# First stage of a transformer layer: modulation and first features as one list schedule, second shift by GpSimd products and ScalarE sums, no transposes of modulation weights

## The chip, the cores and the metric

One core of one Trainium2 chip runs the whole program. The metric is device microseconds of one execution, median of several. The engines are named as in the profile: PE (TensorE matmuls) and PEld (its weight loads), DVE (VectorE), ACT (ScalarE), POOL (GpSimd), SP (SyncE, which issues most DMAs).

## The reference

One layer of a diffusion backbone on 512 latent and 256 context tokens of width 2048, all in float32. What this change touches is the beginning:

```
mod_x = silu(c) @ w_ada + b_ada          # 6 x 2048 numbers: shift, scale, gate, twice
mod_c = silu(c_ctx) @ w_ada + b_ada
h  = rmsnorm(x)   * norm1_w * (1 + scale_x) + shift_x      # latent tokens
hc = rmsnorm(ctx) * norm1_w * (1 + scale_c) + shift_c      # context tokens
p  = h @ w_in;  pc = hc @ w_in
```

Differential attention (8 heads), latent attention (8 heads), the output projection, a gated MLP with a convolution and a last norm follow. The change computes the same numbers.

## The kernel before

Activations stand with features on the 128 partitions and tokens along the free axis: 16 tiles x of 128x512 (latent) and 8 tiles of 128x512, each with two context tiles of 128x256. A tile index is called kt (0 to 15). Float32 products are made from a high part (float32r) and a remainder: `split` copies the high part on ACT (L217) and subtracts on DVE (L218), and `mm3` makes three matmuls, high by high, high by low, low by high (L241 to L243).

The stage in question runs from the start to the end of the first five output tiles, the "first features":

1. Loads of x and ctx (L415, L418). ACT squares them (L435, L437), DVE squares half of the context (L439) and adds all squares up (L441); one matmul with ones sums over partitions (L448) and `rstd` (L293 to L302) gives the reciprocal root `rinv`.
2. silu(c) and silu(c_ctx) are spread over all partitions as `cb` and `ccb` by matmuls with ones (L429) and copies (L443, L445).
3. `modulation(u)` for a pair of tiles, u from 0 to 7. `scales(u)`: 16 matmuls of the padded columns `cpad` with the weight columns `adak` in four column groups of PE (L348), an eviction (L350), two small matmuls with `sel` that add the groups (L352), and L360 on DVE, which gives the factors `a1`. `shifts(kt)`: for an even kt a dot product along the free axis on DVE for c and one for c_ctx, each in two halves of 1024 (L384, an operation that also reads its accumulator); for an odd kt the weight rows `ada` are transposed on PE (L400, 16 of 128x128), evicted by ACT (L401), multiplied as in `scales` and evicted to `modx`, `modc` (L404). The weights of the first features are loaded and split (L227, L217, L218).
4. For each kt: DVE scales the tile (L500), ACT adds the shift and rounds to the high part (L502), DVE makes the remainder (L503), for the latent and for the context tile; then PE makes 27 matmuls (five latent outputs and four context outputs, three each).

Item 1 and 2 are in an order written out by hand; items 3 and 4 are ordered by the framework's priorities. The PSUM of the stage is full: two tiles of two banks and four of one; one of them, `acc`, serves all of modulation.

The attention that comes later is ordered by a planner, the class `Flow`: each step has an engine, a cost, a due time `at` and the buffers it reads and writes; a table `PLAN` shifts the due times of named parts; `run` walks through time, gives each free engine the ready step that is due first, and then emits the steps in that order. Buffers of a ring are given out in order of due times.

Of the kernel before, what the change touches and what calls it, by code (L numbers as in the profile page):

```python
# [9 lines left out]
F32 = mybir.dt.float32  # L10
# [41 lines left out]
class Buf:  # L52


    def __init__(self, flow, ring, make):
        self.ring, self.make, self.tile = ring, make, None
        self.users, self.writers, self.readers, self.left = [], [], [], 0
# [7 lines left out]
class Step:  # L65
    __slots__ = ("eng", "cost", "lag", "at", "fn", "bufs", "left", "next", "takes", "start", "n", "ready")

    def __init__(self, eng, cost, lag, at, fn, n):
        self.eng, self.cost, self.lag, self.at, self.fn, self.n = eng, cost, lag, at, fn, n
        self.bufs, self.left, self.next, self.takes, self.ready = [], 0, [], [], 0.0  # L70
# [10 lines left out]


class Flow:
# [7 lines left out]
    def buf(self, make, ring=None, count=None):  # L91
        if ring and ring not in self.rings:
            self.rings[ring] = (count, [])
        return Buf(self, ring, make)

    def step(self, eng, cost, at, fn, r=(), w=(), needs=(), lag=None):
        at += self.plan.get(self.part, 0.0)
        s = Step(eng, cost, self.LAGS[eng] if lag is None else lag, at, fn, len(self.steps))
# [6 lines left out]
        for b in dict.fromkeys([*r, *w]):  # L105
            if b.ring and not b.users:
                s.takes.append(b)
            b.users.append(s)
            b.left += 1
            s.bufs.append(b)  # L110
# [10 lines left out]
    def run(self):  # L121
# [4 lines left out]
        engines = {"PE": -3.0, "ACT": 2.0, "DVE": 2.8, "POOL": 0.0, "SP": now, "X": -3.0}  # L126
# [6 lines left out]

        for s in self.steps:
            if not s.left:
                event(s.ready)
                open_[s.eng].append(s)
        order = []

        turns = {}  # L140
        for s in sorted(self.steps, key=lambda s: (s.at, s.n)):
            for b in s.takes:
                turns.setdefault(b.ring, []).append(b)

        def free(b):
            count, taken = self.rings[b.ring]
            if turns[b.ring][len(taken)] is not b:
                return False
            return len(taken) < count or taken[-count].left == 0

        event(now)
        for t in set(engines.values()):
            event(t)
        while events:
# [4 lines left out]
            for s in batch:  # L159
                if s is None:  # L160
                    continue
                for b in s.bufs:
                    b.left -= 1
                for n_ in s.next:
# [6 lines left out]
            for e in engines:  # L171
                while engines[e] <= now + 1e-9:
                    can = [s for s in open_[e] if s.ready <= now + 1e-9 and all(free(b) for b in s.takes)]
# [4 lines left out]
                    for b in s.takes:  # L178
                        self.rings[b.ring][1].append(b)
# [10 lines left out]
def layer_kernel(ctx: ExitStack, tc: tile.TileContext, small, rope, c_row, cc_row, x_t, ctx_t, ada, ada_k,  # L190
# [56 lines left out]
    sm.tile([P, 88], F32, name="edge")  # L247
# [77 lines left out]


    zero_d = dram.tile([64, TT], F32, name="zero_d")
# [4 lines left out]
    for c0, c1, r in ((0, 480, slice(0, 64)), (480, TT, slice(64, P))):  # L332
        gp.dma_start(zero_d[:, c0:c1].rearrange("p (k j) -> p k j", j=(c1 - c0) // KT),
                     cpad[r, :, 2:2 + (c1 - c0) // KT])
# [7 lines left out]
    def products(src, n):  # L342


        for j in range(4):
            for c in range(4):
                kt = 4 * j + c
                pe.matmul(acc[32 * c:32 * c + 32, :n], cpad[:, kt], src(kt), start=j == 0, stop=j == 3)  # L348
        row = st.tile([P, 2 * P], F32, tag="row", name=nm("row"), bufs=1)[:, :n]
        sc.copy(row, acc[:, :n])  # L350
        for i in range(n // P):
            pe.matmul(acc[:, 2 * i:2 * i + 2], row[:, i * P:(i + 1) * P], sel, start=True, stop=True)  # L352

    def scales(u, ws=None):

        ws = ws or columns(u)
        products(lambda kt: ws[kt // 4][:, kt % 4], 2 * P)
        for i in range(2):
            kt = 2 * u + i
            ve.tensor_scalar(out=a1[:, 2 * kt:2 * kt + 2], in0=acc[:, 2 * i:2 * i + 2], scalar1=b1[:, kt:kt + 1],  # L360
                             scalar2=col("n1", kt), op0=ALU.add, op1=ALU.mult)

    def columns(u):
        ws = []
        for j in range(4):
# [21 lines left out]
    def shifts(kt):  # L387
# [4 lines left out]
        if kt % 2 == 0:  # L392
            for i in range(2):
                shift(kt, ws, i)
# [1463 lines left out]
```

## Time and profile before

| | |
|---|---|
| median of 3 runs | 2398.79 us (2398.31 to 2403.32) |
| the profiled execution | 2404.97 us |
| its span on the core | 2403.1 us, 33008 instructions |
| PE busy | 2342.3 us (97%) |
| DVE busy | 1701.1 us (71%) |
| ACT busy | 1153.6 us (48%) |
| POOL busy | 336.3 us (14%) |
| DMA | 404.31 MB, mean 168 GB/s |

A row of a group reads: line, engine, operation, output<-inputs, shapes, count, then busy time and mean ns of one, then the idle time of the engine just before and what ended it. A row of a stretch reads: from:to in us, its length, the busy time and the count of each engine, then the granted clock of PE (1.00 is full), the busy share of the DMA engines and GB/s. A row in order of time reads: start, duration, engine, line, operation. An instruction that is issued and then held counts as busy while it is held.

### The profile page before, as it was taken

The numbers are of one execution on the slowest core, as the hardware profiler recorded it, in microseconds if no ns is written. First come the engines' busy times: TensorE is split into PE (matmuls) and PEld (weight loads), VectorE is DVE, ScalarE is ACT, GpSimd is POOL, SyncE is SP. The second block draws the span as 40 slices with busy tenths as digits, with TensorE's granted clock in tenths as the row PEclk, the third lists the DMA queues.
The fourth block names the chain that finished last, engine by engine and source line by source line (L and its number), as shares of the span: only waits on it lengthen the run. The fifth ranks groups of instructions, "written<-read, shape, count | busy, mean of one in ns | idle before, by whom it ended". The sixth has DMA issues, their size and how long they took to land.

```text
span 2403.1 us, 33008 instructions
## 1 busy us (share of the span) xinstructions
PE 2342.3 (97%) x12758; PEld 1981.3 (82%) x12758; DVE 1701.1 (71%) x2244; ACT 1153.6 (48%) x1752; POOL 336.3 (14%) x320
## 2 busy tenths in 40 slices
PE   5999999999999999999999999999999999999997
PEld 3678878887788888798888888888888888888887
DVE  6668886477878766399585757575767676766767
ACT  4333121177776732255454545454545444544546
POOL 0000000155433221100101010101010101111110
PEclk9999999999999999999999999999999999999999
DMA  8867899844521168333646465555554656565573
GB/s 281 295 230 277 304 336 330 269 130 139 156 64 50 34 255 320 131 115 97 144 130 144 128 144 137 140 140 141 132 147 123 153 122 158 123 153 128 140 186 105
DMA packets 132853, 404.31 MB, mean 168 GB/s; under 512 B 14628, under 2 KB 25380, under 8 KB 124244
## 3 DMA queue, kind: packets, MB, share of 16 engines
q1 hardware_dynamic: 106166, 351.66, 44.4%
q0 software_dynamic: 25376, 49.49, 11.9%
q8 instruction: 100, 1.64, 0.3%
q10 hardware_dynamic: 1152, 1.05, 0.1%
q14 instruction: 59, 0.48, 0.1%
HBM read 332.47 MB, written 69.67 MB: 167 GB/s over the span
## 4 chain that ended last, share of the span: by engine, by line
PE 84%; DVE 7%; DMA 4%; ACT 3%; issue 2%; SPq 0%; DVEq 0%; ACTq 0%
PE y L1577 12%; PE b L242 10%; PE b L241 10%; PE b L243 9%; PE z L1577 6%; PE y L1579 6%; PE s L241 3%; PE s L719 3%; PE s L243 3%; PE s L242 3%; PE z L1579 3%; DMA ada<-in_ada 3%; PE x L1577 2%; PE f L241 1%; PE f L242 1%
## 5 line engine op out<-in xcount | busy, mean ns | idle before, releaser
L1598 POOL DMA_DIRECT2D x_d<-xs x160 | 139.9, 1005 | 1161.4 <-ACT xs L1597 1159.5
L1433 DVE TENSOR_TENSOR wl<-wr,wh 128x1024 fp32r<-128x1024 f32 x144 | 176.5, 1225 | 158.6 <-ACT wh L1425 157.9
L1425 ACT CAST wh<-wr 128x1024 fp32r<-128x1024 f32 x144 | 151.1, 1049 | 234.8 <-PE b L242 120.7
L241 PE MATMUL b<-ah,wh 128*128 128x512 f32 (+1 forms) x664 | 256.8, 387 | 0.0
L242 PE MATMUL b<-al,wh 128*128 128x512 f32 (+1 forms) x664 | 256.7, 387 | 0.0
L243 PE MATMUL b<-ah,wl 128*128 128x512 f32 (+1 forms) x664 | 255.9, 385 | 0.0
L1433 DVE TENSOR_TENSOR wl<-rb,wh 128x1024 fp32r<-128x1024 f32 x123 | 150.0, 1220 | 126.8 <-ACT wh L1425 126.8
L1425 ACT CAST wh<-rb 128x1024 fp32r<-128x1024 f32 x123 | 129.3, 1051 | 186.5 <-PE b L242 115.8
L1433 DVE TENSOR_TENSOR wl<-ws,wh 128x1024 fp32r<-128x1024 f32 x123 | 150.1, 1221 | 89.8 <-ACT wh L1425 89.8
L1425 ACT CAST wh<-ws 128x1024 fp32r<-128x1024 f32 x123 | 128.3, 1043 | 130.1 <-PE b L242 45.2
L309 DVE CUSTOM_DVE_ANT_0 ada<-ada,cb,smt 128x2048 f32<-128x2048 f32 x64 | 152.3, 2383 | 46.6 <-DMA ada<-in_ada 46.6
L1577 PE MATMUL y<-a2k,wh 128*128 128x512 f32 x656 | 164.0, 392 | 0.0
L217 ACT CAST wh<-wr 128x1024 fp32r<-128x1024 f32 (+1 forms) x69 | 67.5, 978 | 195.2 <-PE s L243 48.8
L241 PE MATMUL b<-a2k,wh 128*128 128x512 f32 (+1 forms) x376 | 141.7, 377 | 5.9 <-ACT a2k L1282 4.3
L243 PEld LDWEIGHTS b<-ah,wl 128*128 128x128 f32 x664 | 124.8, 188 | 25.7
L241 PEld LDWEIGHTS b<-ah,wh 128*128 128x128 f32 x664 | 125.1, 188 | 22.9
L242 PEld LDWEIGHTS b<-al,wh 128*128 128x128 f32 x664 | 125.1, 188 | 22.0
L242 PE MATMUL b<-a2k,wh 128*128 128x512 f32 (+1 forms) x376 | 140.9, 375 | 0.0
L243 PE MATMUL b<-a2k,wl 128*128 128x512 f32 (+1 forms) x376 | 140.1, 373 | 0.0
L1577 PEld LDWEIGHTS y<-a2k,wh 128*128 128x128 f32 x656 | 118.6, 189 | 21.6
L218 DVE TENSOR_TENSOR wl<-wr,wh 128x1024 fp32r<-128x1024 f32 (+1 forms) x69 | 80.0, 1159 | 46.0 <-ACT wh L217 45.5
L722 DVE TENSOR_REDUCE m<-s 128x1 f32<-128x768 f32 x96 | 91.2, 951 | 28.0 <-PE s L719 27.5
(480 smaller groups left out, 5932.5 us busy)
## 6 DMA issues: line engine op xcount, KB each, us to landing
ada<-in_ada SPq DMA_DIRECT2D x64, 1024.0 KB, 7.0
rb<-in_w_up SPq DMA_DIRECT2D x123, 512.0 KB, 4.3
wr<-in_w_dn SPq DMA_DIRECT2D x88, 512.0 KB, 4.1
x_d<-xs POOLq DMA_DIRECT2D x160, 256.0 KB, 6.0
wr<-in_w_up SPq DMA_DIRECT2D x53, 512.0 KB, 4.2
wr<-in_w_f SPq DMA_DIRECT2D x34, 512.0 KB, 7.3
ada<-in_ada SPq DMA_DIRECT2D x32, 512.0 KB, 7.2
adak<-in_ada_k SPq DMA_DIRECT2D x32, 512.0 KB, 6.3
```

What stands on the lines that cost most here:

```text
L218: ve.tensor_tensor(dst_l, src, dst_h.bitcast(F32), op=ALU.subtract)
L241: pe.matmul(out, st[0], mv[0], start=start, stop=False, **kw)
L242: pe.matmul(out, st[0], mv[1], start=False, stop=False, **kw)
L243: pe.matmul(out, st[1], mv[0], start=False, stop=stop, **kw)
L309: ve.tensor_tensor_reduce(out=junk, in0=w, in1=vec, op0=ALU.mult, op1=ALU.add, scale=1.0, scalar=col("b_ada", j), accum_out=dst[:, j:j + 1])
L719: pe.matmul(s()[:, c0:c1], a, b[:, c0:c1], start=i == 0, stop=i == len(ms) - 1)
L722: step("DVE", 0.87, t + cost + 0.2, lambda: ve.tensor_reduce(out=m(), in_=s()[:, :TT], axis=AX.X, op=ALU.max, negate=True), r=[s], w=[m])
L1425: sc.copy(t, raw[:, k * n_:k * n_ + n_])
L1433: ve.tensor_tensor(t, raw[:, k * n_:k * n_ + n_], hi[k].bitcast(F32), op=ALU.subtract)
L1577: pe.matmul(o, w[j][0], hs[j], start=start and j == 0, stop=False, skip_group_check=True)
L1579: pe.matmul(o[:, h0], w[j][1], hs[j][:, h0], start=False, stop=j == 7, skip_group_check=True)
L1598: gp.dma_start(x1_d[dt], x, accum_op=ALU.add)
```

## The change

**One planned stage.** Items 1 to 4 above become steps of a `Flow` of their own (`flow.part` names: l loads, b spreading, q squares, r the root, a scales, d and p the two shifts, k features), with costs and due times as numbers in the code: T0 = 31 and 6.15 us for each kt. The table `PLAN` has new entries for these parts and changed entries for the attention parts. `Flow.run` takes the engines' starting times as an argument, and a ring's buffer is now given out when any buffer of the ring is free, in order of due times, not when the one that is `count` places back is free.

**The second shift.** For c (shift of the latent tokens) every kt has the dot product on DVE, in two halves. For c_ctx only kt = 0 has it; for kt 1 to 15 POOL multiplies the weight rows by `ccb` in two halves of 128x1024 into tiles `pj` (a ring of 2), ACT sums each along the free axis (an identity with an accumulator), and one small DVE operation adds the halves and `b_ada`. Transposes, their evictions and the second set of products on PE are gone.

**Smaller pieces.** POOL squares the context tiles (16 of 128x256); the last two squares are not added on DVE but go into the matmul with ones; the root's refinement is done for latent and context tokens apart; four copies to `cb` move to ACT and four to `ccb` to DVE; the table of ACT for exp and the small exp stand earlier; the zeros `zero_d` are written from a zeroed tile behind this stage, as rows of 768, and no longer from `cpad` at the start in pieces of 30 and 18 numbers; a padding tile `edge` shrinks from 88 to 24 columns, and the sums `sh` take 64.

The core of the diff:

```diff
+    def shift(kt):
+        ws = rows[kt]
+        t = T0 + PER * kt - 12
+        for i in range(2):
+            at_b[i][kt] = b = buf(lambda: None)
+            d, vec = (modx, modc)[i][:, kt:kt + 1], (cb, ccb)[i]
+            flow.part = f"{'dp'[i]}{kt}"
+            if i and kt:
+                parts_ = []
+                for hf in range(2):
+                    pj = buf(lambda: st.tile([P, 1024], F32, tag="pj", name=nm("pj"), bufs=2), "pj", 2)
+                    o, a = slice(hf * D // 2, (hf + 1) * D // 2), buf(lambda: None)
+                    step("POOL", 2.5, t + 2.5 * hf, lambda hf=hf, pj=pj, o=o: gp.tensor_tensor(
+                        out=pj(), in0=ws[hf](), in1=ccb[:, o], op=ALU.mult), r=[ws[hf], *wide[1]], w=[pj])
+                    step("ACT", 1.0, t + 2.5 * hf + 2.5, lambda hf=hf, pj=pj: sc.activation(
+                        pj(), pj(), AF.Identity, accum_out=sh[:, 2 * kt + hf:2 * kt + hf + 1]), w=[pj, a], lag=0.3)
+                    parts_.append(a)
+                step("DVE", 0.15, t + 6.3, lambda d=d: ve.scalar_tensor_tensor(
+                    out=d, in0=sh[:, 2 * kt:2 * kt + 1], scalar=col("b_ada", kt), in1=sh[:, 2 * kt + 1:2 * kt + 2],
+                    op0=ALU.add, op1=ALU.add), r=parts_, w=[b])
+                continue
+            for hf in range(2):
+                def dot(hf=hf, i=i, d=d, vec=vec):
+                    w = ws[hf]()
+                    junk = st.tile([P, D // 2], BF16, tag="junk", name=nm("junk"), bufs=1)
+                    ve.tensor_tensor_reduce(out=junk, in0=w, in1=vec[:, hf * D // 2:(hf + 1) * D // 2], op0=ALU.mult,
+                                            op1=ALU.add, scale=1.0, scalar=d if hf else col("b_ada", kt), accum_out=d)
+
+                step("DVE", 1.3, t + 3 + 1.3 * hf + 2.6 * i, dot, r=[ws[hf], *wide[i]], w=[b], lag=0.2)
...
-        wt = st.tile([P, KT, P], F32, tag="wt", name=nm("wt"), bufs=1)
-        for q in range(4):
-            for i in range(4):
-                k = (q % 2) * 4 + i
-                pe.transpose(acc[:, i * P:(i + 1) * P], ws[q // 2][:, k * P:(k + 1) * P], ident)
-            sc.copy(wt[:, 4 * q:4 * q + 4].rearrange("p k f -> p (k f)"), acc)
-        products(lambda kt: wt[:, kt], P)
...
+        step("POOL", 0.75, t, lambda q=q, c=c, o=o: gp.tensor_tensor(out=q()[:, T:], in0=c()[:, o], in1=c()[:, o],
+                                                                   op=ALU.mult), r=[c], w=[q])
...
+        flow.run({"PE": 1.0, "ACT": 3.8, "DVE": 5.0, "POOL": 2.0, "SP": 1.0, "X": 0.0})
...
-        flow.run()
+        flow.run({"PE": -3.0, "ACT": 2.0, "DVE": 2.8, "POOL": 0.0, "SP": -100.0, "X": -3.0})
```

How the order moves. POOL's program of before, from its first own instructions on (`ident` is the identity, `cpad` the padded columns, `v_d` the stored values of the attention):

```order
masks.py:197 MEMSET ident 128x128
L331 MEMSET cpad 128x512
masks.py:199 ISA
masks.py:199 AFFINE_SELECT ident<-ident 128x128
L333 DMA zero_d<-cpad 64x16x30
L333 DMA zero_d<-cpad 64x16x18
L652 DMA v_d_137<-v_3770 128x4x128
```

And POOL's program of the change, where the squares of the context (`h` from `c2k`) give way to the products (`pj` from weight rows `ada` and the spread `ccb`):

```order
L418 TENSOR_TENSOR h_319<-c2k_276 128x256
L418 TENSOR_TENSOR h_327<-c2k_276 128x256
L520 TENSOR_TENSOR pj_375<-ada_342,ccb 128x1024
L520 TENSOR_TENSOR pj_392<-ada_350,ccb 128x1024
L520 TENSOR_TENSOR pj_408<-ada_365,ccb 128x1024
L520 TENSOR_TENSOR pj_434<-ada_380,ccb 128x1024
```

POOL had nothing between zero_d's writes and the stored values; now it has 16 squares and 30 products there, and zero_d's write stands behind them.

DVE's program of before, in the middle of the stage, one pair of tiles: `wl` are remainders of weights, `a2k` and `c2k` of features, `h` scaled tiles, ISA is the dot product and the reading of its accumulator:

```order
L218 TENSOR_TENSOR wl_642<-wr_639,wh_641 128x640
L218 TENSOR_TENSOR wl_694<-wr_691,wh_693 128x640
L384 ISA junk_775,modx<-ada_771,cb,smt 128x1024
L384 ISA modx 128x1
L384 ISA ada_771,modc<-ada_771,ccb,smt 128x1024
L384 ISA modc 128x1
L384 ISA junk_777,modx<-ada_773,cb,modx 128x1024
L384 ISA modx 128x1
L404 TENSOR_SCALAR modx<-b_334,smt 128x1
L404 TENSOR_SCALAR modc<-b_334,smt 128x1
```

The same place in the change:

```order
L533 ISA junk_793,modx<-ada_743,cb,modx 128x1024
L533 ISA modx 128x1
L533 ISA junk_805,modx<-ada_760,cb,modx 128x1024
L533 ISA modx 128x1
L475 TENSOR_TENSOR wl_818<-wr_772,wh_803 128x640
L525 SCALAR_TENSOR_TENSOR modc<-sh,smt 128x1
L556 SCALAR_TENSOR_TENSOR h_831<-a2k_213,a_91,rinv 128x512
L561 SCALAR_TENSOR_TENSOR a2k_842<-h_788,modx,a2k_823 128x512
L556 SCALAR_TENSOR_TENSOR h_788<-c2k_207,a_91,rinv 128x256
L533 ISA junk_858,modx<-ada_795,cb,smt 128x1024
```

Every dot is now one with `cb` into `modx`, for even and odd tiles; `modc` comes from the sums `sh` by one small operation.

PE's program of before, between the first features of two tiles (`wh` and `wl` weights, `b` and `s` PSUM tiles; `ident` marks the transposes):

```order
L400 MATMUL b_334<-ident,ada_645 128x128 x4
L242 MATMUL b_331<-a2k_736,wh_521 128x512
L243 MATMUL b_331<-a2k_735,wl_522 128x512
L241 MATMUL s_425<-a2k_871,wh_641 128x512
L241 MATMUL s_426<-a2k_871,wh_641 128x512
L400 MATMUL b_334<-ident,ada_645 128x128 x4
L242 MATMUL s_425<-a2k_872,wh_641 128x512
```

And in the change:

```order
L488 MATMUL b_322<-adak_525,cpad 32x256 x4
L247 MATMUL s_422<-a2k_554,wh_510 128x512
L248 MATMUL s_422<-a2k_571,wh_510 128x512
L249 MATMUL s_422<-a2k_554,wl_534 128x512
L488 MATMUL b_322<-adak_539,cpad 32x256 x4
```

Between features only the matmuls for the scales are left.

More of the change, by code (lines that the diff above doesn't have):

```diff
@@ L119, in step, with run @@
         return s
-    def run(self):
+    def run(self, begin):
         import heapq
         now = -100.0
-        engines = {"PE": -3.0, "ACT": 2.0, "DVE": 2.8, "POOL": 0.0, "SP": now, "X": -3.0}
+        engines = dict(begin)
         open_ = {e: [] for e in engines}
@@ L138, in run @@
         order = []
[L140 to L143, printed above, removed]
         def free(b):
[L146 to L153, printed above, removed]
+            return not b.ring or b.taken or turns[b.ring][0] is b and live[b.ring] < self.rings[b.ring]
         while events:
@@ L172, in run @@
                 while engines[e] <= now + 1e-9:
-                    can = [s for s in open_[e] if s.ready <= now + 1e-9 and all(free(b) for b in s.takes)]
+                    can = [s for s in open_[e] if s.ready <= now + 1e-9 and all(free(b) for b in s.bufs)]
                     if not can:
@@ L354, in scales @@
[L354 to L365, printed above, removed]
-            wk = st.tile([P, 4, 2 * P], F32, tag="adak", name=nm("adak"), bufs=4)
-            nc.sync.dma_start(wk, ada_k[u, j // 2][:, (j % 2) * 4:(j % 2) * 4 + 4])
-            ws.append(wk)
-        return ws
@@ new lines, in layer_kernel @@
+    for kt in range(KT):
+        features(kt)
+    flow.part = "l"
+    load(T0 + 30, 200, lambda: nc.sync.dma_start(ropet, rope), [buf(lambda: None)])
+    step("SP", 0.4, T0 + 20, lambda: nc.sync.dma_start(silu_c, cb[0:1]), r=[rows_[0]])
+    with tc.manual_schedule(engines={mybir.EngineType.PE, mybir.EngineType.Activation, mybir.EngineType.DVE,
+                                     mybir.EngineType.SP, mybir.EngineType.Pool}):
+        flow.run({"PE": 1.0, "ACT": 3.8, "DVE": 5.0, "POOL": 2.0, "SP": 1.0, "X": 0.0})
@@ L510, in layer_kernel @@
+    lat0, ctx0 = [lat0(f) for f in range(5)], [ctx0(f) for f in range(4)]
     st.release()
```

365 lines of the change are left out of this document (226 added, 139 removed), and 21 rows, old and new, of the table PLAN.

## The prediction

> **What bounds the kernel now.** I read the profile from the whole to the place. The section on the 40 slices shows TensorE (PE) at 90% or more in all but the first and the last; the change works in the first three. So the next view was the busy time by stretches, cut where the stages change.
>
> ```profile
> core 0: us, PE busy (x) PEld busy (x) DVE busy (x) ACT busy (x) POOL busy (x), PEclk, DMA share, GB/s
> 0.00:35.00 35.00, 14.02 (x16) 5.15 (x16) 20.21 (x38) 20.46 (x33) 3.07 (x9) 1.00 0.95 284
> 49.00:184.00 135.00, 132.93 (x1073) 95.44 (x1072) 86.78 (x169) 50.56 (x98) 0.00 (x0) 0.98 0.74 263
> ```
>
> For 35 us PE waits for inputs and their squares; from 49 to 184 us it is busy for 132.9 of 135 us, while VectorE (DVE) has 86.8 us of work and GpSimd (POOL) none. The chain that ended last and PE's instructions in order of time give the two edges:
>
> ```profile
> 34.26 0.96 DVE sqs L441
> 35.26 2.92 PE s L448 x4
> ...
> 49.30 1.22 PE s L241 x2
> ```
> ```profile
> 183.71 0.39 PE L243 MATMUL b<-a2k,wl 128*128 128x512 f32 x1
> ```
>
> The stage is over at 183.71 + 0.39 = **184.1 us**. What follows, down to the end at 2403.1, starts from there, so the change is worth what it does to this number. PE's modulation work in the stage, grouped by form:
>
> ```profile
> L400 PE MATMUL b<-ident,ada 128*128 128x128 f32 x128 | 22.0, 298 | 4.0 <-issue 2.0 <-ACT wt L401 1.4 <-DVE a L360 0.6
> L348 PE MATMUL b<-adak,cpad 128*32 128x256 f32 x256 | 21.2, 415 | 0.0
> L348 PE MATMUL b<-wt,cpad 128*32 128x128 f32 x256 | 9.5, 294 | 0.0
> ...
> L352 PE MATMUL b<-sel,row 128*128 128x2 f32 x48 | 6.7, 233 | 1.0 <-ACT row L350 1.0
> ```
> ```profile
> 94.59 0.57 PE b L348 x8
> ...
> 111.36 0.57 PE b L348 x8
> ```
>
> **What the change takes from PE.** The transposes (22.0 us), the products on transposed weights (9.5) and 8 of the 24 small matmuls behind them (a third of 6.7) go: about 33 us that stood on the bounding engine, 4.2 of the 16.8 us that a pair of feature tiles takes (the last two rows, from the chain, open successive pairs). On ScalarE (ACT) the evictions of those transposes go; 30 sums over 128x1024 come. The write of zero_d moves from the first microseconds behind the stage, where no one needs it for 200 us.
>
> **What it adds.** Thirty products of 128x1024 on POOL (L520), two for each of the feature tiles 1 to 15, and 16 squares of 128x256. DVE keeps its load: it loses the second dot product of 7 even tiles and gains the first of 8 odd ones (34 dots of 1024 instead of 32), its 16 splits of weights, 64 feature operations and most of the additions of squares. In the stage of before POOL never ran, so whether the two engines can work side by side has to be read further on, where both run. There the rows speak plainly. DVE, then POOL, at 883 us:
>
> ```profile
> 883.16 2.34 DVE L309 CUSTOM_DVE_ANT_0 ada<-ada,cb,smt 128x2048 f32<-128x2048 f32 x1
> ...
> 885.43 2.30 DVE L218 TENSOR_TENSOR wl<-wr,wh 128x1024 fp32r<-128x1024 f32 x1
> 887.65 3.38 DVE L309 CUSTOM_DVE_ANT_0 ada<-ada,cb,smt 128x2048 f32<-128x2048 f32 x1
> ```
> ```profile
> 883.45 3.20 POOL L1152 TENSOR_TENSOR ss<-ss,sq 128x512 f32<-128x512 f32 x1
> ...
> 887.16 1.72 POOL L1152 TENSOR_TENSOR ss<-ss,sq 128x512 f32<-128x512 f32 x1
> ```
> ```profile
> L1152 POOL TENSOR_TENSOR ss<-ss,sq x11: 1292/1724/3199, 881.4 to 973.6; 128x512 f32<-128x512 f32 x11
> ```
>
> POOL's sum takes 1.29 us at best, here 3.20: it starts at 883.45, the dot product ends at 885.50, the sum ends at 886.65, that is 1.15 later. The split L218, begun at 885.43, ends at 887.73, 1.08 behind POOL's end. Then POOL again 1.15 behind that, and the next dot at 891.03, 2.15 behind 888.88. They take **strict turns**, and each counts what it costs behind the other's end. The same with the wider form and with the short ones:
>
> ```profile
> L871 POOL TENSOR_TENSOR p<-p,p x32: 1833/1850/2484, 485.0 to 667.3; 128x768 f32<-128x768 f32 x32
> ```
> ```profile
> 519.13 2.48 POOL L871 TENSOR_TENSOR p<-p,p 128x768 f32<-128x768 f32 x1 [0.29 <-ACT p L870]
> ```
> ```profile
> 518.62 1.30 DVE L683 TENSOR_TENSOR wl<-wr,wh 128x1024 fp32r<-128x1024 f32 x1
> 519.83 0.95 DVE L722 TENSOR_REDUCE m<-s 128x1 f32<-128x768 f32 x1
> 521.03 0.69 DVE L702 TENSOR_TENSOR wtl<-pt,wth 128x512 fp32r<-128x512 f32 x1 [0.25 <-ACT wth L695]
> ```
>
> POOL's 128x768 sum waits for the split's end at 519.92 and ends 1.69 later (alone: 1.83 at best). The reduction L722 and L702, whose inputs lie in PSUM, wholly or in part, run beside it at their usual length. So those DVE instructions block that read two tensors from SBUF, and in this stage that is nearly all of them: the dots (L533), the splits (L475), the feature products and remainders (L556, L561), the additions of squares (L423).
>
> Here the Trainium skill disagrees with itself, and the choice decides the sign. "Advanced Engine Details and Errata", section Mode Summary, names only DVE's instructions in a 2-port mode as those that GpSimd blocks; by that sentence alone the dots would run beside the products, and the result would be the first rival below. "SBUF — State Buffer", section SBUF: two separate sides, adds instructions with two SBUF inputs and says that the pair is held for the whole instruction; the sum would then be the one that follows. The rows above agree with the second: 3.20 and 3.38 us instead of 1.29 and 2.34.
>
> **The sum of the shared turns.** DVE's prices alone, from its groups in the stage of before:
>
> ```profile
> L441 DVE TENSOR_TENSOR sqs<-sqs,sq 128x768 f32<-128x768 f32 x15 | 14.3, 956 | 2.2 <-ACT sq L437 1.2
> L218 DVE TENSOR_TENSOR wl<-wr,wh 128x640 fp32r<-128x640 f32 x16 | 13.2, 822 | 1.1 <-ACT wh L217 0.9
> L503 DVE SCALAR_TENSOR_TENSOR a2k<-h,modx,a2k 128x512 fp32r<-128x512 f32 x16 | 12.0, 748 | 1.8 <-ACT a2k L502 1.8
> L500 DVE SCALAR_TENSOR_TENSOR h<-a2k,a,rinv 128x512 f32<-128x512 f32 x16 | 11.2, 745 | 0.0
> L384 DVE CUSTOM_DVE_ANT_0 junk<-ada,cb,modx 128x1024 bf16<-128x1024 f32 x8 | 10.3, 1283 | 0.1
> ...
> L503 DVE SCALAR_TENSOR_TENSOR c2k<-h,modc,c2k 128x256 fp32r<-128x256 f32 x16 | 7.7, 479 | 0.5 <-ACT c2k L502 0.5
> ...
> L384 DVE DVE_READ_ACCUMULATOR2_ANT modx<- 128x1 f32 x16 | 1.3, 84 | 0.0
> ```
>
> POOL's 128x1024 product is in no row. Its two forms step by 0.54 us per 256 columns (1.15 to 1.69 behind a wait, 1.29 to 1.83 alone), so an estimate is 2.25 behind a wait and 2.39 alone; the 128x256 square is 0.60 or 0.74 in the same way. DVE behind a wait: 1.08 for 1024 columns gives, in proportion, 0.82 (768), 0.69 (640), 0.55 (512), 0.28 (256) and 1.08 for a dot of half 2048.
>
> - Low end, everybody behind a wait: 13 additions 10.7, 16 squares 9.6, 34 dots 36.7, 16 splits 11.0, 32 wide and 32 narrow feature operations 26.6, the six of the root's refinement 2.5, 30 products 67.5: **165 us**.
> - High end, everybody at its price alone: 12.4, 11.8, 34 x (1.28 + 0.08) = 46.2, 13.2, 39.2, 2.9, 71.7: **197 us**.
>
> DVE has some 130 such instructions and POOL 46, so only about a third of DVE's stand behind a wait: DVE's 113.9 less a third of the 26.4 between its ends is 105, and 7 less for successive instructions that overlap by 0.08: 98. POOL lies in the middle of its ends, 80. Together **178 us**.
>
> This starts when the first x tile lands. ACT squares it at 10.3 us now, while zero_d's small pieces fill the DMA engines (share 0.81 at 170 GB/s in the first 10 us); without them I take 8, and it can hardly be before 5.
>
> ```profile
> 0.00:10.00 10.00, 2.79 (x4) 1.23 (x5) 1.15 (x11) 6.14 (x5) 3.07 (x9) 1.00 0.81 170
> ...
> 30.00:40.00 10.00, 4.74 (x24) 2.14 (x28) 8.44 (x12) 5.69 (x11) 0.00 (x0) 1.00 1.02 408
> 40.00:50.00 10.00, 6.03 (x38) 3.69 (x31) 7.23 (x14) 4.06 (x9) 0.00 (x0) 0.72 0.33 117
> 50.00:60.00 10.00, 10.00 (x73) 7.81 (x71) 7.45 (x17) 2.38 (x5) 0.00 (x0) 0.77 1.01 366
> ```
>
> Three small terms: 8 us in which the pair is free because DVE waits for ACT's high part (0.66 us at 178 us now) once for each of 8 pairs of tiles, or for a load; 5 us at the end, since PE now ends 4.9 us behind the last L503; and 5 us for PE's clock. The last two rows show why: after PE has sat idle, the granted clock is down to 0.72 and 0.77. After the change PE has no more than 12.5 us of work for each pair of tiles that costs DVE and POOL nearly 20, so it idles some us in each and will partly run at a lower clock; nothing to perhaps 10 us comes of it.
>
> ```profile
> 178.06 0.75 DVE L503 SCALAR_TENSOR_TENSOR a2k<-h,modx,a2k 128x512 fp32r<-128x512 f32 x1 [0.66 <-ACT a2k L502]
> 178.72 0.48 DVE L503 SCALAR_TENSOR_TENSOR c2k<-h,modc,c2k 128x256 fp32r<-128x256 f32 x1
> ```
>
> The stage then ends at 8 + 178 + 8 + 5 + 5 = 204 us instead of 184: **20 us later**.
>
> What is behind the waits: ACT's sum L522 waits for its product, and behind it on ACT stand high parts (L559) for which DVE and then PE wait; a loaded half row comes free only when both the dot and the product have read it, so SP's queue waits there too. Both are in the 8 us; ACT's own load (50.6 us of 135 before) hides the 30 sums. The loads themselves, 45 MB, take 113 us at 400 GB/s (408 between 30 and 40 us) and are covered. The attention schedule gets another table but no other instructions; PE waits 6.2 us there for L702 and for that I take nothing, with 6 us to either side:
>
> ```profile
> PE po L242 <- DVE wtl L702: 4.3, 3, 1.8
> ...
> PE pt L739 <- DVE wtl L702: 1.9, 2, 1.5
> ```
>
> **Reference.** The profiled execution took 2404.97 us with a span of 2403.1; it would become 2425. The median of the runs shown is 2398.79, so the forecast is **2419 us**.
>
> **Rivals.**
> 1. *The products run beside DVE.* Then DVE's own work would count: from 33 us on 30 dots, splits, features and the root at their prices alone, 96, less 9 of overlaps, 7 of small ones, 8 of waits and 5 for PE: 140. PE itself would start some 7 us before the present 49, without the first pair's transposes, and take 8 x 12.5: 142. The stage ends 42 us earlier: 2357. It decides as soon as a product and a dot stand beside each other at 2.4 and 1.28 us. For it: no row shows a 1024-wide product. Against it: every row above. Chance 0.10.
> 2. *PE's clock becomes the bound.* At half clock a pair costs PE 25 us against 20 of the shared turns. It decides from three quarters of the time at half clock; at nine tenths a pair takes 12.5 / 0.55 = 22.7, and 50 + 8 x 22.7 + 5 = 237: 2452. Against it: a PE with work in hand gets its clock back, as after 60 us. Chance 0.07.
> 3. *The low end.* Turns at 165 us, start at 7, free for 5, 5 at the end: 182, some 2 us before the present end, 2397; up to 2404. Chance 0.08.
>
> **How the numbers follow.** The forecast's own case (2404 to 2438) has 0.75. A run of this kernel can be told from no change beyond 0.2%, 4.8 us. Faster: 0.10 of rival 1 and 0.02 of rival 3, 0.12; same 0.06; slower 0.82. The range 2400 to 2442 leaves out rival 1, rival 2 and a bit of rival 3.
>
> **What would show it.** In the changed profile L520 would have a mean well over 2.4 us (about 3) and the dots over 1.28, starting and ending in turns; DVE over 90% and POOL about 60% busy from 40 to 195 us; PE near 65% with clocks under 1; the first-feature matmuls ending near 204 us. If L520 shows 2.4 and the dots 1.28 side by side, or if the stage ends before 180 us, I am wrong.

## The result, and the profile after

The changed kernel takes 2434.97 us (median of 4 runs, 2428.16 to 2438.79) against 2398.69 us (2398.31 to 2403.32): a ratio of 1.0144 with a 95% interval of 1.0118 to 1.017, 36 us slower. (Ratios below are against the kernel before, with this interval in brackets.) Measured again beside other runs of the kernel before it gave 1.0128 [1.0112, 1.0145] (e12 below). The forecast was slower by 20, in a range that holds the result.

The profiled execution has a span of 2437.0 us, 33.9 over the 2403.1 of before. Three edges of the program, which every kernel of this study has, cut this into parts. PE's last instruction of the first features in the changed kernel (start, duration):

```profile
204.50 0.28 PE L249 MATMUL b<-c2k,wl 128*128 128x256 f32 x1
```

They end at 204.8 us, where it was 184.1: **20.7 us later**, the prediction's 20. The second edge is DVE's 41st dot product of the next stage (L309 before, L315 in the change), the third POOL's last store of x1. Of before, then of the change:

```profile
404.46 2.35 DVE L309 CUSTOM_DVE_ANT_0 ada<-ada,cb,smt 128x2048 f32<-128x2048 f32 x1
...
1016.19 0.54 POOL L1491 DMA_DIRECT2D x_d<-b2k  x1 [4.92 <-DVE b2k L1175]
```
```profile
427.38 2.35 DVE L315 CUSTOM_DVE_ANT_0 ada<-ada,cb,smt 128x2048 f32<-128x2048 f32 x1 [0.71 <-DMA ada<-in_ada]
...
1051.53 0.54 POOL L1597 DMA_DIRECT2D x_d<-b2k  x1 [4.92 <-DVE b2k L1281]
```

From the first to the second edge it takes 222.6 us instead of 220.4; from the second to the third, where the attention and its projection lie, 624.1 instead of 611.7, **12.4 us more**; behind it 1385.5 instead of 1386.9. That is 20.7 + 2.2 + 12.4 - 1.4 = 33.9. So two things have to be explained: the stage that the prediction worked out, and a loss of half that size where it took nothing.

**The stage.** Busy time in the changed kernel by stretches; the third row is the prediction's 40 to 195 us, the last goes from the first square (ACT, 5.43 us) to the end of the last L561 (DVE):

```profile
core 0: us, PE busy (x) PEld busy (x) DVE busy (x) ACT busy (x) POOL busy (x), PEclk, DMA share, GB/s
50.00:100.00 50.00, 40.81 (x225) 29.43 (x226) 49.39 (x57) 21.21 (x39) 25.98 (x10) 0.82 0.72 246
100.00:150.00 50.00, 39.72 (x219) 28.43 (x217) 46.11 (x53) 17.84 (x33) 26.38 (x10) 0.83 0.70 251
...
40.00:195.00 155.00, 117.21 (x645) 82.36 (x642) 147.76 (x173) 61.17 (x114) 77.11 (x30) 0.83 0.64 221
```
```profile
5.43:199.06 193.63, 144.69 (x716) 95.12 (x717) 178.34 (x206) 81.97 (x144) 95.63 (x48) 0.86 0.69 244
```

The bounding engine has changed: DVE is busy for 147.8 of 155 us (95%) where it had 86.8 of 135, and PE, 132.9 of 135 before, now waits a quarter of the time. For about a third of its busy time DVE is held in an instruction that it has started. One pair of products on POOL, in the middle of the stage, and DVE's instructions beside them:

```profile
97.87 2.41 POOL L520 TENSOR_TENSOR pj<-ada,ccb 128x1024 f32<-128x1024 f32 x1 [6.91 <-ACT pj L522]
```
```profile
100.23 3.38 POOL L520 TENSOR_TENSOR pj<-ada,ccb 128x1024 f32<-128x1024 f32 x1
```
```profile
97.99 3.38 DVE L533 CUSTOM_DVE_ANT_0 junk<-ada,cb,smt 128x1024 bf16<-128x1024 f32 x1
101.30 0.08 DVE L533 DVE_READ_ACCUMULATOR2_ANT modx<- 128x1 f32 x1
101.30 0.46 DVE L502 TENSOR_SCALAR a<-b,b,smt 128x2 f32<-128x2 f32 x2
101.68 2.49 DVE L556 SCALAR_TENSOR_TENSOR h<-a2k,a,rinv 128x512 f32<-128x512 f32 x1
104.09 1.27 DVE L533 CUSTOM_DVE_ANT_0 junk<-ada,cb,modx 128x1024 bf16<-128x1024 f32 x1
```

Read the ends. The first product ends at 100.28, the dot that began beside it at 101.37, 1.09 later. The second product, begun at 100.23, ends at 103.61, 2.24 behind the dot. L556, begun at 101.68, ends at 104.17, 0.56 behind the product. L502, which takes its input from PSUM, passes at its usual length while the second product runs. The next dot, without a product beside it, takes 1.27. Those are the prediction's turns and its prices behind a wait: 1.08, 2.25 and 0.55.

The whole stage is like this pair. Of the 129 dots, splits, feature operations and L525 on DVE, 29 take more than 1.3 times the shortest of their form, 60.6 us more in all. Every one of the 29 ends behind a product of POOL, and always by the same time for its form: 1.08 us (1024 columns), 0.68 (640), 0.55 (512), 0.28 (256), 0.01 to 0.02 (L525). The stage of e5 below, with the products out, has none of these, and that of e2 a single one, of 0.1 us.

Over the whole stage, POOL's and DVE's groups:

```profile
L520 POOL TENSOR_TENSOR pj<-ada,ccb 128x1024 f32<-128x1024 f32 x30 | 82.2, 2751 | 73.7 <-ACT pj L522 68.0 <-DMA ada<-in_ada 5.7
```
```profile
L533 DVE CUSTOM_DVE_ANT_0 junk<-ada,cb,smt 128x1024 bf16<-128x1024 f32 x15 | 27.5, 1836 | 0.1
L533 DVE CUSTOM_DVE_ANT_0 junk<-ada,cb,modx 128x1024 bf16<-128x1024 f32 x16 | 24.6, 1535 | 0.1
...
L525 DVE SCALAR_TENSOR_TENSOR modc<-sh,smt 128x1 f32<-128x1 f32 x15 | 18.2, 1213 | 0.6 <-ACT pj L522 0.6
```

The products take 2.75 us on the mean, the dots 1.84 and 1.54 instead of 1.28. POOL's idle time stands behind `ACT pj L522`, which looks like the cause (POOL waits for ACT's sum to free one of two tiles); e2 and e3 had to tell whether it is.

### The profile page after: what moved, and what is told of

The parts are those of the page before. It is cut to its first block, busy times and chain, and to the rows that moved or that the text cites. A ratio compares the mean times of both kernels' runs of the same rounds, so it can differ in the third digit from the quotient of the medians.

```text
span 2437.0 us, 32321 instructions
## 1 busy us (share of the span) xinstructions
PE 2340.2 (96%) x12366; PEld 1977.0 (81%) x12366; DVE 1770.0 (73%) x2241; ACT 1162.2 (48%) x1766; POOL 427.8 (18%) x366
## 3 DMA queue, kind: packets, MB, share of 16 engines
q0 software_dynamic: 25328, 49.49, 11.5%
q10 hardware_dynamic: 1152, 1.05, 0.1%
## 4 chain that ended last, share of the span: by engine, by line
PE 77%; DVE 12%; DMA 4%; issue 4%; ACT 3%; SPq 0%; DVEq 0%; ACTq 0%
PE y L1683 12%; PE b L247 9%; PE b L248 9%; PE b L249 9%; PE z L1683 6%; PE y L1685 6%; PE s L823 3%; PE z L1685 3%; DMA ada<-in_ada 3%; PE s L249 2%; PE s L248 2%; PE s L247 2%; PE x L1683 2%; PE f L247 1%; PE f L248 1%
## 5 line engine op out<-in xcount | busy, mean ns | idle before, releaser
L1531 ACT CAST wh<-wr 128x1024 fp32r<-128x1024 f32 x144 | 151.0, 1049 | 231.2 <-PE b L248 119.9
L315 DVE CUSTOM_DVE_ANT_0 ada<-ada,cb,smt 128x2048 f32<-128x2048 f32 x64 | 152.3, 2381 | 51.2 <-DMA ada<-in_ada 51.0
L223 ACT CAST wh<-wr 128x1024 fp32r<-128x1024 f32 x53 | 55.8, 1052 | 188.3 <-DMA wr<-in_w_o 45.5
L828 ACT ACTIVATE p<-s,m 128x768 f32<-128x768 f32 x96 | 86.7, 904 | 45.5 <-DVE m L826 42.2
```

Of the source, the lines that this page charges most:

```text
L315: ve.tensor_tensor_reduce(out=junk, in0=w, in1=vec, op0=ALU.mult, op1=ALU.add, scale=1.0, scalar=col("b_ada", j), accum_out=dst[:, j:j + 1])
L828: step("ACT", 0.9, t + cost + 1.2, lambda: sc.activation(p(), s()[:, :TT], AF.Exp, bias=m(), accum_out=lcol()), r=[s, m], w=[p, l], lag=0.25)
L1531: sc.copy(t, raw[:, k * n_:k * n_ + n_])
```

## The experiments

The theory of the stage: strict turns of POOL's products and DVE's two-input instructions set its length. Its rivals: the ring of two product tiles with ACT's sums behind them; the list schedule itself; the mere number of DVE's instructions. For the rest of the program: the new order of the attention, or loads that landed late in one execution.

### e2: the products cut to 16 columns

```
-  out=pj(), in0=ws[hf](), in1=ccb[:, o], op=ALU.mult), r=[ws[hf], *wide[1]], w=[pj])
+  out=pj()[:, :16], in0=ws[hf]()[:, :16], in1=ccb[:, o.start:o.start + 16], op=ALU.mult), ...
...
-  pj(), pj(), AF.Identity, accum_out=sh[:, 2 * kt + hf:2 * kt + hf + 1]), w=[pj, a], lag=0.3)
+  pj(), ws[hf](), AF.Identity, accum_out=sh[:, 2 * kt + hf:2 * kt + hf + 1]), r=[ws[hf]], w=[pj, a], lag=0.3)
```

> GpSimd's products cover 16 columns of each 1024 (the rest is left out, so the second shift is not the reference's); ScalarE's sums keep their length and read the weight rows. Turns theory: each product shrinks from 2.3 to about 0.25 us, 30 of them give back 60 us, until the next bound (VectorE's own load or TensorE, about 140 us) stops it: first features end at 140 to 155, dots back at 1.28 us, time about 2375. Rival (ScalarE's queue and the ring of two product tiles hold GpSimd up, not the turns): the sums are as long as before, so the stage ends at 185 or later.

Measured: 2374.81 us (2371.65 to 2375.09), ratio 0.989 [0.9875, 0.9905]; the features end at 147.5. Its stretches:

```profile
50.00:100.00 50.00, 50.00 (x361) 37.27 (x360) 44.82 (x88) 32.48 (x59) 5.16 (x13) 1.00 0.99 373
100.00:150.00 50.00, 47.49 (x307) 36.05 (x305) 40.05 (x77) 27.47 (x52) 6.69 (x14) 1.00 0.75 275
```

POOL's instructions became short (0.38 us at the median), and 57 us of the stage went. The ring of two tiles and the order of instructions on every engine stayed, and so did the 30 sums on ACT with their length (1.05 us), but for what they read: the weight rows instead of the product tile. POOL still sat idle 46.8 us for them. PE is busy for 50.00 of 50 us again at full clock. The ring and ACT's sums are refuted as the cause.

### e5: POOL writes as much, but reads nothing

```
-  step("POOL", 2.5, t + 2.5 * hf, lambda hf=hf, pj=pj, o=o: gp.tensor_tensor(
-      out=pj(), in0=ws[hf](), in1=ccb[:, o], op=ALU.mult), r=[ws[hf], *wide[1]], w=[pj])
+  step("POOL", 2.5, t + 2.5 * hf, lambda hf=hf, pj=pj, o=o: gp.memset(
+      pj(), 1.0), r=[ws[hf], *wide[1]], w=[pj])
```

> Leaves out the 30 products: GpSimd fills pj with a constant over the same 128x1024 instead (it writes as much and reads nothing from SBUF); ScalarE's sums and all waits stay. If VectorE's two-input instructions shut out any GpSimd instruction that writes SBUF, each fill takes a turn of about 1 us: the dots show over 1.4 us on the mean and the first features end 15 to 25 us later than with the 16-column products (147.5), at 163 to 173. If only GpSimd's reading counts, the fills run beside the dots (1.28 us) and the features end at 145 to 152.

Measured (one run): 2377.93 us, features end at 148.9. POOL's group, one fill in order of time, and DVE beside it:

```profile
L520 POOL MEMSET pj<- 128x1024 f32 x30 | 28.5, 953 | 73.9 <-ACT pj L522 73.9
```
```profile
84.62 0.96 POOL L520 MEMSET pj<- 128x1024 f32 x1 [3.10 <-ACT pj L522]
```
```profile
84.88 0.48 DVE L556 SCALAR_TENSOR_TENSOR h<-c2k,a,rinv 128x256 f32<-128x256 f32 x1
85.27 1.28 DVE L533 CUSTOM_DVE_ANT_0 junk<-ada,cb,smt 128x1024 bf16<-128x1024 f32 x1
```

The fill runs from 84.62 to 85.58; L556 lies wholly inside it and the dot begins inside it, both at the length that they have alone. So POOL's writing does not shut DVE out; its reading does. It need not read two tensors: in the kernel before, POOL's L868 reads one tensor and two columns. Beside it, on POOL and then on DVE:

```profile
495.39 1.48 POOL L868 TENSOR_SCALAR p<-p,rl,neglam 128x768 f32<-128x768 f32 x1 [2.32 <-DVE rl L867]
```
```profile
495.31 2.09 DVE L829 SCALAR_TENSOR_TENSOR qs<-rt,qs 64x512 fp32r<-64x512 f32 x2
```

The two of L829, which take 0.69 us each alone, read two tensors. L868 ends at 496.87, the second of L829 at 497.40, 0.53 later.

### e3: three product tiles

```
-  pj = buf(lambda: st.tile([P, 1024], F32, tag="pj", name=nm("pj"), bufs=2), "pj", 2)
+  pj = buf(lambda: st.tile([P, 1024], BF16, tag="pj", name=nm("pj"), bufs=3), "pj", 2)
```

> A ring of three product tiles in place of two, in bfloat16 to fit (so the second shift is rounded); order of instructions unchanged. Turns theory: the shared turns stay the same sum, the stage ends within 4 us of 204.8. Rival (the 68 us that GpSimd sat idle for ScalarE's sums, a full ring, are what costs): the stage ends 15 us or more earlier.

Measured: 2430.31 us (2429.02 to 2436.51), ratio 1.0129 [1.0114, 1.0145]; features end at 202.7, 2.1 earlier.

```profile
L520 POOL TENSOR_TENSOR pj<-ada,ccb x30: 2339/2710/3542, 33.7 to 182.9; 128x1024 bf16<-128x1024 f32 x30
...
  ACT pj L522: 40.0, 13
```

POOL's wait for ACT fell from 68.0 to 40.0 us, and the stage, 2.1 us shorter, did not follow: it was idle time of POOL that nearly no one waited for.

### e1: the shifts of c as dots on DVE

```
-            if i and kt:
+            if i and kt > KT:
```

> The changed kernel with the second shift back on VectorE: for every feature tile both shifts are dot products on VectorE, GpSimd makes no products; the list schedule and everything else stay. Turns theory (GpSimd's product and VectorE's instructions with two SBUF inputs take turns): 30 products of 2.25 to 2.4 us leave the shared turns and 30 dots of 1.28 + 0.08 come, 70 us out and 41 in, so the first features end 20 to 30 us before the changed kernel's 204.8 us (175 to 185), and the time is about 2410. Rival (nothing but VectorE's own load counts, products ran beside it): 41 us more on VectorE, the stage ends at about 245 and the time is 2475.

Measured: 2424.22 us (2421.65 to 2434.49), ratio 1.0109 [1.0082, 1.0137]; features end at 199.1, which neither theory had. The dots are at 1.28 again, as the turns ask, but DVE has 30 more of them, and the planned order puts them where PE needs DVE for something else. PE's waits from 50 to 150 us and the stretches:

```profile
PE b L488 <- DVE a L502: 16.0, 5, 8.6
PE b L488 <- DMA adak<-in_ada_k: 15.1, 8, 4.6
```
```profile
50.00:100.00 50.00, 35.17 (x238) 23.73 (x236) 43.20 (x75) 8.89 (x16) 0.00 (x0) 0.78 0.83 296
100.00:150.00 50.00, 26.71 (x159) 15.33 (x160) 44.96 (x78) 6.09 (x12) 0.00 (x0) 0.62 0.69 248
150.00:199.00 49.00, 49.00 (x275) 42.84 (x273) 32.33 (x56) 14.19 (x23) 1.49 (x2) 1.00 0.32 105
```

PE has 26.7 us of work in 50 and then 49 of 49: the work came late, behind DVE and behind loads of `adak` alike. The run does not price the dots alone: the due times of the list were made for products on POOL.

### e6 and e9: the odd tiles' weights in the layout that the products want

In the kernel before, without its schedule changed (e6): the odd tiles' shift weights are read in k-major layout (stored with the index that is summed over on the partitions), so that PE multiplies them directly.

```
-  for q in range(4):
-      for i in range(4):
-          k = (q % 2) * 4 + i
-          pe.transpose(acc[:, i * P:(i + 1) * P], ws[q // 2][:, k * P:(k + 1) * P], ident)
-      sc.copy(wt[:, 4 * q:4 * q + 4].rearrange("p k f -> p (k f)"), acc)
-  products(lambda kt: wt[:, kt], P)
+  for q in range(2):
+      t = st.tile([P, KT // 2, P], F32, tag="wt", name=nm("wt"), bufs=3)
+      nc.sync.dma_start(t, ada_s[kt // 2, q])
+      wt.append(t)
+  products(lambda kt: wt[kt // 8][:, kt % 8], P)
```

> The kernel before, with the shift weights of the odd feature tiles kept in the layout that the products on TensorE want, so that the transposes and their evictions go and nothing is moved to VectorE or GpSimd. If TensorE's own work was the bound and GpSimd's products are what made the change lose, the stage loses nearly the 22.0 us of transposes, less what the first pairs wait for loads: features end at 155 to 168 us, and the time is 2370 to 2388. The rival, that loads are what the stage would then wait for (the same 45 MB in less time): features end at 172 to 182, 2388 to 2398.

Measured: 2400.08 us (2396.43 to 2407.66), ratio 0.9987 [0.9976, 0.9997]; features end at 180.4. My figure was wrong. The rival's held for the features (its time, up to 2398, was just passed), but not for its reason: PE waits for no load. Its stretch over the stage and its waits:

```profile
49.00:180.40 131.40, 120.01 (x919) 82.82 (x918) 85.05 (x168) 33.65 (x65) 0.00 (x0) 0.98 0.70 251
```
```profile
PE s L241 <- ACT a2k L501: 7.0, 8, 1.6
PE b L348 <- DVE a L360: 4.4, 7, 0.6
```

PE's busy time fell by 12.9 us, not 22.0: the records of the transposes overlap with their neighbours (only 8.7 us of that stretch are covered by transposes alone). And PE now idles 11.4 us where it idled 2.1, so 3.6 are left. Its program stands in a written order, and with the transposes gone nothing is between PE and these two waits.

The same weights in the changed kernel's list schedule (e9), with even tiles' shifts as dots and no products on POOL. The table's entries for scales, shifts and features, made for the products, are dropped, and the dots are due 2 us earlier:

```
-  if i and kt:
-      ...
-      step("POOL", 2.5, t + 2.5 * hf, lambda hf=hf, pj=pj, o=o: gp.tensor_tensor(
+  if kt % 2:
+      ...
+      step("PE", 0.45, t + 3 + 0.5 * j, products, r=[ws[j // 2], pad], w=[acc])
```

> The changed kernel with its list schedule, but the odd tiles' shifts go back to TensorE, on weights kept in the layout that the products want; the even tiles' shifts stay dots on VectorE; no products on GpSimd, no sums on ScalarE. If the shared turns are what the change lost by, and not the list schedule, the dots are at 1.28 us and the features end at 148 to 165 us; the later stages stay as with the change, so the time is 2380 to 2397. If the list schedule itself loses, the features end above 175 us.

Measured: 2398.44 us (2392.51 to 2401.42), ratio 0.9973 [0.9962, 0.9983]; features end at 169.8. One of its four groups of dots (the others 1.28 to 1.31 us):

```profile
L544 DVE CUSTOM_DVE_ANT_0 junk<-ada,ccb,modc 128x1024 bf16<-128x1024 f32 x8 | 10.3, 1282 | 0.2
```

So planning the stage as a list is not what lost: with the products taken off POOL it ends the stage 14.3 us before the old one and 35 before the change. 169.8 is 5 above my bound, and the time 1.4 above its own. And 14.3 us earlier in the stage became only about 5 in the time: the rest of the program gave 9 back, as with the change.

### e8: zero_d written at the start again

```
+  zero_d = dram.tile([64, TT], F32, name="zero_d")
+  for c0, c1, r in ((0, 480, slice(0, 64)), (480, TT, slice(64, P))):
+      gp.dma_start(zero_d[:, c0:c1].rearrange("p (k j) -> p k j", j=(c1 - c0) // KT),
+                   cpad[r, :, 2:2 + (c1 - c0) // KT])
```

> The changed kernel with zero_d written at the start in small pieces as in the kernel before. If the start term was right (the small pieces cost the first x tile some us), the squares begin 2 to 4 us later and the features end 2 to 4 us later than with the change, at 207 to 209. If the first pieces cost nothing: 203 to 206.

Measured (one run): 2431.91 us; features end at 206.1, 1.3 later, between the two. The first squares of the change, then of e8:

```profile
5.43 0.63 ACT L416 ACTIVATE h<-a2k 128x512 f32<-128x512 f32 x1
...
7.90 1.28 ACT L416 ACTIVATE h<-a2k 128x512 f32<-128x512 f32 x2
```
```profile
5.29 0.61 ACT L420 ACTIVATE h<-a2k 128x512 f32<-128x512 f32 x1
...
11.11 0.63 ACT L420 ACTIVATE h<-a2k 128x512 f32<-128x512 f32 x1 [3.41 <-DMA a2k<-in_x_t]
```

The small pieces hold up the second x tile by 3.2 us, not the first. Whether the stage loses its 1.3 us by that is not settled: e8 was executed once, and two executions of the change ended the stage 0.3 us apart (204.8 and 205.1).

### e4, e11, e12: the rest of the program

e4 is the changed kernel with the attention in the old order; e11 is the kernel before with the attention in the new one; e12 is the changed kernel unedited. The order is more than the table: the class with its rule for rings and two PSUM tiles allocated ahead go with it.

```
e4:
-    flow = Flow(PLAN)
+    flow = OldFlow(OLD_PLAN)
...
-    b_tile("po", 1)
-    b_tile("f", 1)
e11:
-        flow.run()
+        flow.run({"PE": -3.0, "ACT": 2.0, "DVE": 2.8, "POOL": 0.0, "SP": -100.0, "X": -3.0})
...
+    b_tile("po", 1)
+    b_tile("f", 1)
```

In e4 the old class and table are taken over beside the new ones; in e11 the new ones stand in place of the old.

> The changed first stage with the attention ordered by the table and the ring rule of before. If the attention's new order costs something, the span from the end of the first features (204.8 us) to the end (2232 us in the changed kernel, 2219 before) shrinks by up to 13 us. If the 13 us are loads that land differently in stages whose code did not change, it stays within the spread of the changed kernel's runs, 2428 to 2439.

> The kernel before with one thing changed: the attention is put in order by the new class and table, with the two PSUM tiles allocated ahead, as in the change. If the table costs about 5 us, the ratio is 1.0015 to 1.003, the first-to-last x1 store takes 139 to 141 us instead of 136, and the features end at 184 as before. If it costs nothing, as the prediction took, the ratio is within 0.999 to 1.001.

> The changed kernel once more, unedited, for its spread and a second profile. The features end at 203 to 207 again. If the 10 us that its first profile lost between the features and the first scores belong to the change, this stretch takes 303 to 306 again; if it was that execution's loads, it takes 297 to 300.

Measured: e4 2427.44 us (2424.24 to 2431.08), ratio 1.0113 [1.0098, 1.0128]; e11 2414.92 us (2412.88 to 2418.72), ratio 1.0057 [1.0044, 1.007]; e12 2432.66 us (2428.79 to 2437.24). The features end at 203.3, 182.7 and 205.1. **The new order alone costs 13.7 us in the kernel before** (10.6 to 16.8), more than I had read from e4; the first to the last store of x1 takes 141.8 us, just over the 139 to 141 that I had. The profile of e11 is of the fastest of its six executions and shows 8.0 of them. From the features to the end e4 takes 2223.6 us, 8.6 less than the change's first profile, but only 1.3 less than e12's: e4 alone decides nothing. The stretch between the second and third edges, before, e11, the change, e12, e4:

```profile
404.50:1016.20 611.70, 604.28 (x3039) 504.88 (x3038) 423.78 (x572) 324.26 (x564) 192.77 (x151) 1.00 0.48 160
```
```profile
400.90:1024.10 623.20, 608.92 (x3039) 505.84 (x3039) 429.79 (x572) 324.46 (x564) 191.28 (x150) 0.99 0.47 157
```
```profile
427.40:1051.50 624.10, 607.43 (x3036) 505.16 (x3035) 429.35 (x571) 324.28 (x564) 190.65 (x150) 0.99 0.47 157
```
```profile
426.10:1044.40 618.30, 605.12 (x3035) 504.02 (x3034) 429.09 (x571) 324.35 (x564) 191.12 (x151) 1.00 0.47 159
```
```profile
425.60:1040.50 614.90, 605.56 (x3039) 505.32 (x3038) 422.24 (x572) 324.23 (x564) 192.82 (x151) 0.99 0.48 159
```

The same work (before and e11 both show 3039 matmuls), but other waits: PE idles 7.4 us before, 14.3 in e11, 16.7 in the change, 13.2 in e12, 9.3 in e4. PE's waits in this stretch of the change; of before the prediction shows the two that count (4.3 us in 3 times, 1.9 in 2):

```profile
PE po L248 <- DVE wtl L806: 6.3, 7, 1.8
PE s L247 <- DVE nr L224: 2.8, 1, 2.8
PE s L249 <- DVE wl L224: 2.4, 2, 2.2
PE pt L843 <- DVE wtl L806: 1.9, 2, 1.5
PE s L249 <- DVE wl L787: 1.5, 1, 1.5
PE s L823 <- ACT p L828: 1.2, 2, 0.7
```

Seven of the low parts of transposed weights (L806, L702 before) come late for `po` instead of three, and four waits for splits are new (L224, L787). Of e11's 11.5 us, 6.9 are such idle time; the other 4.6 are PE busy longer over the same matmuls, at a granted clock of 0.99. From the features to the first reduction over scores e12 took 298.2 us, the change's first profile 304.6, before 294.9: about 6 of the 624.1 were that execution's. 2.8 of them are the one wait for `nr`, which e12 does not have. By e12's expectation they were its loads; no row here shows that.

### e10: k-major weights, the list, and the attention as before

This is e9 with e4's edit.

> The list schedule with the odd tiles' shifts on TensorE in k-major weights (as in e9), and the attention in the order of the kernel before. If the new attention table costs about 5 us, as e4's stretches show, the features end near 170 and the time is 2391 to 2397, that is 0.9945 to 0.9975 of the kernel before. If the table costs nothing, it stays at e9's 0.9973 or above.

Measured: 2394.07 us (2390.97 to 2397.17), ratio 0.9967 [0.9955, 0.998] against the kernel before; features end at 169.4. It is faster than both kernels, by 8 and by 39 to 41 us. Whether the old order helped here can't be told from the times: the interval overlaps with e9's. The profiles tell more when the stretch between the second and third edges is cut at DVE's first reduction over scores. Length and PE's idle time in us, on each side of it:

| attention | kernel | up to it, idle | behind it, idle |
|---|---|---|---|
| old order | before | 74.6, 0.0 | 537.1, 7.4 |
| | e6 | 75.8, 2.5 | 536.4, 8.2 |
| | e4 | 80.4, 3.4 | 534.5, 5.9 |
| | e10 | 81.5, 7.0 | 535.9, 7.3 |
| new order | e11 | 78.2, 0.0 | 545.1, 14.3 |
| | the change | 82.1, 2.8 | 542.1, 13.9 |
| | e12 | 77.2, 0.0 | 541.1, 13.2 |
| | e9 | 78.2, 0.0 | 544.1, 14.0 |

Behind the cut PE idles 6 to 8 us in all four kernels with the old order and 13 to 14 in these four with the new, whatever the first stage is (11.6 to 14.5 in e1, e2, e3, e5 and e8). So the new order's waits cost some 6 us with either first stage. Up to the cut the new order does more work early (342 to 346 matmuls instead of 330) and, of these four, idles in the change's first profile alone. There e4 and e10 lose 3.4 and 7.0 us by one and three waits for splits on DVE, and this hides what the old order gives them behind the cut.

## Why the prediction was right, and where it was not

- **The bound and the change of sign: right.** Strict turns were read from rows of another stage, with other forms, and held for a product that no row had shown. The kernels that shorten the products or put fills in their place (e2, e5) end the stage at 147.5 and 148.9; one with a third tile (e3) ends it at 202.7. The 60.6 us in which DVE is held are the size of what e2 gives back (57). Here the traces side with the Trainium skill's "SBUF — State Buffer", section SBUF: two separate sides: an instruction of DVE with two SBUF inputs and one of GpSimd that reads SBUF exclude each other for the whole instruction. A dot of 3.38 us beside a product, and of 1.28 beside a fill, agree. The note in the Trainium skill's "Advanced Engine Details and Errata", section Mode Summary, names the 2-port instructions alone, and that dot is what it leaves out.
- **The sum of 178: it held, its neighbours less well.** DVE stands in instructions for 178.34 us between the first square and the last L561. The split is not quite mine. Counted as I counted, without DVE's small instructions and evictions but with the time in which POOL alone holds the pair, it is 178.0. Yet this hides two sizes that I had otherwise: about a quarter of DVE's two-input instructions stand behind POOL (I had a third), and L525, which I had not listed, takes 18.2 us. Then: start 5.4 (I had 8), DVE idle 15.3 (8), end 5.7 (5), clock nothing of its own (5): 5.4 + 178.3 + 15.3 + 5.7 = 204.7. The idle time was twice what I took, and the start and the clock paid for it. Part of the good hit at 204.8 is luck. The start was also read wrongly: in the kernel before ACT came to the first square at 10.27 us behind two activations for silu and a table load (5.26 to 10.25), and in e8, with zero_d's small pieces back, it came at 5.29. That zero_d's pieces held it is not shown.
- **The clock: there, but hidden.** PE's granted clock is 0.82 and 0.83. Little time can follow, since DVE, which bounds the stage, waits for PE only twice in it, 2.6 us each. I had said PE would be near 65% busy; it is 117.2 of 155, 76%: at that clock the same 748 matmuls of the stage cover 150.4 us, and 126.7 in e2 at the clock near 1.00 that it has from 50 us on. POOL is at 77.1 of 155, 50%, where I had said 60.
- **What failed** is the sentence on the attention: "for that I take nothing, with 6 us to either side". The new order costs 11.5 to 12.4 us in the profiles of e11 and the change, 6.6 in e12's, 13.7 in e11's times. That is most of the difference between the 20 of the forecast and the 30 to 36 measured. I looked for it where PE waited before (6.2 us) and saw little to lose; but a new order loses by waits that the old one did not have.
- **Rival 1** had 2357. With the products nearly free (e2) the stage ends at 147.5 instead of its 142: the matmuls for scales and features cover 106.3 us in e2, 13.3 for each pair and not 12.5, and their features begin at 45.4. The time is 2374.81 with the new order's loss in it. Rivals 2 and 3 did not come about.

What stays open: some 6 us of the new order's cost are PE's waits behind the first reduction, with either first stage. Why e11 costs 13.7 us in its times is not shown beyond that: 4.6 us of its stretch are PE busy longer over the same matmuls. Nor was it tried which part of the order (table, rule for rings, two tiles allocated ahead) makes the waits, or why e4 and e10 wait for splits before that reduction.

## What to carry to other kernels

Before work is moved from PE to "idle" GpSimd, look in the trace for any stretch in which GpSimd reads SBUF while VectorE reads two tensors from it, and compare ends, not starts: if they take turns, the two engines are one for that work, and the moved work is added to the busier of them. When a later stage is put in a new order with the change, run the old program with that order alone, and cut its time at points that all kernels share; unchanged instructions are no sign of an unchanged price. And work that is taken off the bounding engine (e6) pays only as far as nothing stood behind it that it had covered.

## What the runs showed of the hardware that I had not expected

- A DVE instruction on 128x1 elements waits a whole product out if its two inputs are in SBUF. Of the 15 of L525, 7 take 2.30 to 2.43 us and end 0.01 to 0.02 us behind a product. The other 8 have no product beside them and take 0.20 to 0.22, such as:

```profile
107.36 0.21 DVE L525 SCALAR_TENSOR_TENSOR modc<-sh,smt 128x1 f32<-128x1 f32 x1
```

- GpSimd's fill of 128x1024 (0.95 us), which only writes, takes no turn (e5); its product of the same size (2.34 us at best) does.
- A PE that is starved is granted as little as 0.62 of its clock over 50 us in which it has 26.7 us of work (e1), and 1.00 in the next 49, in which it has work throughout.
